# A two-block transformer kernel: engine queues ordered by a timeline simulation

## The chip, the cores and the metric

The kernel runs on one core of a Trainium2 chip. The metric is the device time of one execution in microseconds (us); the profile comes from one further execution on the same kind of chip. The core's engines are named as in the profile: PE (matrix multiply, with PEld for its weight loads), DVE (vector), ACT (scalar and activation), POOL (GpSimd), and SP, which only issues DMAs. Each engine works through its own queue in a fixed order.

## What is computed

Two blocks follow one another on 512 tokens of width 1024, in float32. Cut to what matters:

```python
# first block
h = modulate(rms_norm(x, norm1_g), shift1, scale1)
q, k, v, g_ret, u, sv, gate_a, gate_b = split(h @ w_in)
branch_a = (silu(g_ret) * head_norm(retention(rotary(q), rotary(k), v))) @ w_ret_out
branch_b = spatial_gating(gelu(u), gelu(sv)) @ w_sgu_out
x = x + gate1 * ((sigmoid(gate_a) * branch_a + sigmoid(gate_b) * branch_b) @ w_out)
h2 = modulate(rms_norm(x, norm2_g), shift2, scale2)
x = rms_norm(x + gate2 * peer(h2), final_g)
# peer, per token: top 16 of 128 x 128 experts in each of 8 heads
act = gelu(h2 . expert_u[expert]) * softmax(top_s)
out = sum(act * expert_v[expert])
# second block, two layers: window attention, latent attention and a gated
# convolution, merged; a context of 256 tokens goes through the first layer
```

## The kernel before

Every float32 product is made of three fp32r products: an operand is split into a high part (ACT, line 105) and a low part (POOL or DVE, line 107), and PE adds high x high, low x high and high x low (lines 80 to 82). Weights stream in over SP's queue (`load`, line 72) into small rings of buffers, are split, and are used once.

The work has these stages. The profile's times for them are rounded to 100 us.

- `first_mixer` (to about 550 us) and then `experts`. In `experts` three streams of work are written into one another. `route` finds the 16 experts of each head. `up_products` multiplies the first 384 tokens by all 16,384 rows of `expert_u` (tile `u`, weights `wr`, `wh`, `wl`, result `hb`). `context` runs the 256 context tokens through the first layer of the second block (tile `cm`, weights `wrc`, `whc`, `wlc`).
- The last 128 tokens are handled differently (`gathered`, line 663 on). For each of 128 (head, rank) pairs POOL issues a gather of one row per token from `expert_u` and one from `expert_v` (line 684, 256 gathers, 128 x 1024 each) into `sg`, a ring of `SG = 4` buffers. A DVE operation reads each: a dot product (line 197) for an `expert_u` row, and an addition into `sacc` (line 699) for an `expert_v` row. A buffer is free for the next gather when its DVE operation is done.
- From about 1900 us the loop over `expert_v` runs: 32 rounds of four weight tiles `vr`, split on ACT and DVE, eight accumulators `acc` on PE (lines 594 to 625), until about 2500 us.
- `second` runs the two layers of the second block (2500 us to the end): per layer, window attention with the convolution's and the gates' products written into it, latent attention, gates, merge.

What sets the order of the queues: the kernel is written with the Tile framework. The source emits instructions in one program order. The author interleaves streams in it by hand with counters: `tick(R1)` to `tick(R6)` emit a part of a filler stream for each step of a main stream, and `sparse(S2)`, `sparse(S3)`, `sparse(S4)`, `sparse(SU)`, `sparse(S5)` (lines 656 to 661) emit one gather step for each unit of due count. `S5 = 0.85` per weight tile of the `expert_v` loop asks for 0.85 x 128 = 109 of the 256 steps inside that loop, if that many are left. When the context closes, Tile plays the whole program through a simulator with a clock: each time an engine is free in that simulation, it is given, of its instructions whose inputs are ready and whose buffers are free, the one that comes first in the source. The order in which each engine received its instructions becomes its queue. So the simulator's clock decides where the queues leave the source's order. On the chip the queue is fixed: an instruction that is not ready holds up all that stands behind it on its engine.

The context is opened in `kernel`, line 1819; `body` calls `Kern(...).build()`.

## Time and profile before

| what | us |
|---|---|
| median of 3 runs | 3908.92 (3907.82 to 3917.36) |
| the profiled execution's own time | 3920.43 |
| its span, first to last instruction | 3918.7 |
| PE busy in the span | 3484.4 (89%) |
| DVE busy | 2363.8 (60%) |
| POOL busy | 1622.9 (41%) |
| ACT busy | 1590.1 (41%) |

The profiled execution is 11.5 us longer than the median of the runs, and 1.7 us longer than its span. Durations below come from that execution. A wait in the profile is the idle time of an engine ahead of an instruction, put down to what ended it. `x` counts instructions. The granted clock of PE is given as a share of its full rate.

### The profile page before, as it was taken

The page shows a single profiled execution, that of the slowest core. Times are in us where ns is not written, and L with a number is a line of the kernel's source. Part 1 is how long each engine was busy: PE and PEld are TensorE (multiplying, and loading weights), DVE is VectorE, ACT ScalarE, POOL GpSimd, SP SyncE. Part 2 cuts the span into 40 slices and gives each one's busy share as a digit, 9 for nine tenths or more (in the row PEclk, how much of TensorE's full clock was granted, in tenths as well). Part 3 has the DMA queues.
Part 4 walks back from the last instruction along what each step waited for, and adds up shares of the span by engine and source line. Part 5 has one row for each costly group of instructions (what it writes and reads, how often), then busy time and mean ns, then how long its engine had stood idle before and what let it go on. Part 6 is the DMA issues. An engine that isn't in the chain of part 4 may idle for free.

```text
span 3918.7 us, 54792 instructions
## 1 busy us (share of the span) xinstructions
PE 3484.4 (89%) x20243; PEld 3124.0 (80%) x20243; DVE 2363.8 (60%) x4567; ACT 1590.1 (41%) x2976; POOL 1622.9 (41%) x1248
## 2 busy tenths in 40 slices
PE   5999999979878777768999999699999998999998
PEld 4888787878768776767899999687877787777787
DVE  7556545799878786876377555544425554442554
ACT  3322233336633354443433333344426643452563
POOL 4454544451256777675300000155424435543342
PEclk9999999989989887888999999699999998999999
DMA  6346324347888886776789766222221232212113
GB/s 240 132 176 249 124 92 146 107 148 278 295 292 283 315 267 234 274 243 229 257 310 324 244 222 215 77 82 70 66 74 51 89 110 72 71 65 77 50 61 107
DMA packets 271947, 667.91 MB, mean 170 GB/s; under 512 B 25280, under 2 KB 87104, under 8 KB 268736
## 3 DMA queue, kind: packets, MB, share of 16 engines
q1 hardware_dynamic: 219248, 469.30, 35.0%
q0 software_dynamic: 36864, 134.23, 10.1%
q10 hardware_dynamic: 15568, 60.89, 4.1%
q8 instruction: 159, 2.61, 0.3%
q14 instruction: 108, 0.88, 0.1%
HBM read 601.34 MB, written 62.98 MB: 170 GB/s over the span
## 4 chain that ended last, share of the span: by engine, by line
PE 56%; DVE 14%; DMA 10%; issue 9%; POOL 5%; ACT 4%; SPq 0%; POOLq 0%; DVEq 0%; ACTq 0%
PE mm L80 5%; PE mm L81 5%; PE mm L82 5%; PE acc L82 4%; PE acc L81 4%; PE acc L80 4%; PE gm L80 3%; PE gm L81 3%; PE gm L82 3%; DMA sg<-ev,xid 3%; POOL sg L684 2%; PE pv L1083 2%; DMA sg<-ur,xid 2%; POOL wl L107 2%; PE tp L1053 2%
## 5 line engine op out<-in xcount | busy, mean ns | idle before, releaser
L107 POOL TENSOR_TENSOR wl<-wr,wh 128x512 fp32r<-128x512 f32 (+3 forms) x418 | 687.0, 1660 | 472.8 <-ACT wh L105 459.9
L105 ACT CAST wh<-wr 128x512 fp32r<-128x512 f32 (+4 forms) x536 | 348.0, 666 | 512.6 <-PE mm L81 169.7
L80 PE MATMUL u<-hh,wh 128*128 128x384 f32 (+1 forms) x1032 | 369.8, 358 | 34.3 <-ACT hb L711 32.2
L82 PE MATMUL u<-hh,wl 128*128 128x384 f32 (+1 forms) x1032 | 366.2, 355 | 28.6 <-POOL wl L107 16.8
L81 PE MATMUL u<-hl,wh 128*128 128x384 f32 (+1 forms) x1032 | 363.0, 352 | 0.0
L81 PE MATMUL acc<-al,vh 128*128 128x384 f32 (+2 forms) x1056 | 353.1, 335 | 0.1
L82 PE MATMUL acc<-ah,vl 128*128 128x384 f32 (+2 forms) x1056 | 353.0, 335 | 0.0
L80 PE MATMUL acc<-ah,vh 128*128 128x384 f32 (+2 forms) x1056 | 352.8, 335 | 0.0
L105 ACT CAST vh<-vr 128x1024 fp32r<-128x1024 f32 x128 | 134.7, 1052 | 344.3 <-DMA vr<-ev 227.8
L80 PE MATMUL mm<-hh,wh 128*128 128x512 f32 (+2 forms) x608 | 242.0, 401 | 33.1 <-ACT wh L105 23.6
L107 DVE TENSOR_TENSOR vl<-vr,vh 128x1024 fp32r<-128x1024 f32 x128 | 158.5, 1239 | 168.5 <-ACT vh L105 158.8
L684 POOL DMA_INDIRECT sg<-ur,xid x128 | 169.6, 1325 | 213.7 <-DVE sg L197 155.2
L81 PE MATMUL mm<-hl,wh 128*128 128x512 f32 (+2 forms) x608 | 243.2, 400 | 3.3 <-POOL hl L107 3.1
L82 PE MATMUL mm<-hh,wl 128*128 128x512 f32 (+2 forms) x608 | 242.4, 399 | 1.4 <-POOL wl L107 1.4
L80 PEld LDWEIGHTS u<-hh,wh 128*128 128x128 f32 x1032 | 206.9, 201 | 39.0 <-ACT hb L711 34.5
L898 POOL TENSOR_TENSOR acc<-acc,sf 128x256 f32<-128x256 f32 x8 | 6.0, 754 | 558.5 <-ACT sf L895 550.3
L82 PEld LDWEIGHTS u<-hh,wl 128*128 128x128 f32 x1032 | 205.3, 199 | 35.2 <-POOL wl L107 20.2
L197 DVE SCALAR_TENSOR_TENSOR wm<-wm,row 128x1024 f32<-128x1024 f32 x120 | 183.0, 1538 | 72.1 <-DMA wm<-wmod 57.4
L699 DVE SCALAR_TENSOR_TENSOR sacc<-sg,wts,sacc 128x1024 f32<-128x1024 f32 x128 | 189.0, 1476 | 50.4 <-DMA sg<-ev,xid 49.6
L80 PE MATMUL cm<-ch,whc 128*128 128x256 f32 (+1 forms) x584 | 178.0, 306 | 46.0 <-DVE cmt L970 17.5
L684 POOL DMA_INDIRECT sg<-ev,xid x128 | 166.5, 1301 | 125.8 <-DVE sacc L699 84.0
L197 DVE SCALAR_TENSOR_TENSOR sg<-sg,htok 128x1024 f32<-128x1024 f32 x128 | 178.7, 1397 | 59.4 <-DMA sg<-ur,xid 59.3
(726 smaller groups left out, 10256.1 us busy)
## 6 DMA issues: line engine op xcount, KB each, us to landing
wr<-eu SPq DMA_DIRECT2D x256, 256.0 KB, 3.4
vr<-ev SPq DMA_DIRECT2D x128, 512.0 KB, 4.5
wm<-wmod SPq DMA_DIRECT2D x88, 512.0 KB, 5.7
wrc<-w SPq DMA_DIRECT2D x83, 512.0 KB, 5.3
wr<-wA SPq DMA_DIRECT2D x80, 512.0 KB, 4.0
wr<-w SPq DMA_DIRECT2D x156, 256.0 KB, 2.6
wrg<-w SPq DMA_DIRECT2D x104, 256.0 KB, 2.6
hd<-hb ACTq DMA_DIRECT2D x64, 384.0 KB, 4.1
```

What stands on the lines that cost most here:

```text
L80: mm(ps, lh, rh, start=first, stop=False)
L81: mm(ps, lh, rl, start=False, stop=False)
L82: mm(ps, ll, rh, start=False, stop=last)
L105: nc.scalar.copy(hi, x)
L107: eng.tensor_tensor(lo, x, hi.bitcast(F32), op=OP.subtract)
L197: self.nc.vector.scalar_tensor_tensor(chunk, chunk, 1.0, row, op0=OP.mult, op1=OP.mult, accum_out=dst)
L684: nc.gpsimd.indirect_dma_start(t, None, tabs[i], bass.IndirectOffsetOnAxis(idx[:, j:j + 1], 0))
L699: nc.vector.scalar_tensor_tensor(acc, t, wts[:, j:j + 1], acc, op0=OP.mult, op1=OP.add)
L898: eng.tensor_tensor(acc[1], acc[1], sf, op=OP.add)
L1053: nc.tensor.transpose(t[:, (b - i) * 128:(b - i + 1) * 128], p[:, b * 128:(b + 1) * 128], self.ident)
L1083: nc.tensor.matmul(o[:, lo:hi], v(b), pt[k][:, b, lo:hi], start=i == 0 and k == 0, stop=i == len(parts) - 1 and k == 1)
```

## The change

```diff
@@ -1816,7 +1816,7 @@
     nc = bacc.Bacc("TRN2", target_bir_lowering=False, num_devices=1)
     a = {n: nc.dram_tensor(n, v.shape, mybir.dt.from_np(v.dtype), kind="ExternalInput").ap() for n, v in arrays.items()}
     out = nc.dram_tensor("out", (128, 8, T), F32, kind="ExternalOutput").ap()
-    with tile.TileContext(nc) as tc:
+    with tile.TileContext(nc, schedule_with_timeline_sim=True) as tc:
         body(tc, a, out, {})
     r = run_bass_kernel_spmd(nc, [arrays], core_ids=[0])
     y = r.results[0]["out"]
```

One argument is added. The source of the program, its tiles, rings and instructions stay as they are. The simulation that gives each engine its order is played on Tile's timeline simulator in place of its plain one. The library calls the timeline simulator the more detailed of the two: it keeps occupancy for engines, sequencers and DMA engines, and it counts a fixed cost of POOL's elementwise instructions that the plain one leaves out. Each queue's order, the buffer that each tile gets, and the semaphore waits that follow from both are worked out anew.

## Rows read from the trace of the kernel before

**Rows 1.** The page: busy time, share of the span and instructions, by engine.

```profile
PE 3484.4 (89%) x20243; PEld 3124.0 (80%) x20243; DVE 2363.8 (60%) x4567; ACT 1590.1 (41%) x2976; POOL 1622.9 (41%) x1248
```

**Rows 2.** Busy time by stage: window, length, engines, granted PE clock, DMA share, GB/s.

```profile
0.00:100.00 100.00, 60.30 (x266) 47.36 (x267) 75.31 (x123) 35.17 (x51) 48.06 (x27) 0.95 0.65 242
100.00:900.00 800.00, 736.74 (x4050) 653.98 (x4049) 503.15 (x1366) 242.93 (x388) 381.47 (x193) 0.95 0.42 147
900.00:1900.00 1000.00, 785.03 (x5192) 738.11 (x5191) 756.70 (x1117) 455.04 (x806) 568.98 (x444) 0.89 0.78 270
1900.00:2500.00 600.00, 590.67 (x3401) 589.07 (x3402) 367.97 (x546) 217.07 (x319) 32.54 (x26) 0.98 0.72 247
2500.00:2600.00 100.00, 64.87 (x444) 60.24 (x444) 40.34 (x99) 35.31 (x72) 45.32 (x39) 0.77 0.30 100
2600.00:3918.00 1318.00, 1246.77 (x6895) 1035.25 (x6895) 620.30 (x1318) 604.60 (x1343) 546.56 (x521) 0.98 0.23 74
```

**Rows 3.** The same table for 1100 to 1900 us alone.

```profile
1100.00:1900.00 800.00, 610.40 (x3855) 577.02 (x3853) 580.09 (x835) 331.82 (x637) 528.49 (x411) 0.88 0.76 264
```

**Rows 4.** The same table for instructions on `sg` alone: DVE, then POOL.

```profile
900.00:1900.00 1000.00, 359.96 (x374) 324.31 (x247) 0.89 0.78 270
1900.00:2500.00 600.00, 0.00 (x0) 0.00 (x0) 0.98 0.72 247
```

**Rows 5.** Longest waits of 900 to 1900 us: total us, times, longest.

```profile
POOL sg L684 <- DVE sg L197: 154.8, 39, 22.9
POOL sg L684 <- DVE sacc L699: 99.0, 35, 14.3
...
DVE sg L197 <- DMA sg<-ur,xid: 59.3, 31, 7.3
...
DVE sacc L699 <- DMA sg<-ev,xid: 49.6, 26, 5.0
```

**Rows 6.** Tile `sg`, 900 to 1900 us: ns min/median/max, first and last start; landing.

```profile
L684 POOL DMA_INDIRECT sg<-ev,xid x128: 933/1119/2278, 951.2 to 1803.5; - x128
L699 DVE SCALAR_TENSOR_TENSOR sacc<-sg,wts,sacc x128: 1264/1283/6228, 1001.2 to 1812.6; 128x1024 f32<-128x1024 f32 x128
L197 DVE SCALAR_TENSOR_TENSOR sg<-sg,htok x123: 1203/1221/5260, 912.8 to 1759.6; 128x1024 f32<-128x1024 f32 x123
...
DMA to landing us min/median/max: 4.1/6.3/12.8
```

**Rows 7.** Instructions in order of time, 1560 to 1570 us: start, us, what, wait.

```profile
1563.32 0.94 POOL L684 DMA_INDIRECT sg<-ev,xid  x1 [0.30 <-issue]
...
1567.09 1.28 DVE L699 SCALAR_TENSOR_TENSOR sacc<-sg,wts,sacc 128x1024 f32<-128x1024 f32 x1 [5.00 <-DMA sg<-ev,xid]
...
1568.29 0.41 DVE L972 SCALAR_TENSOR_TENSOR u<-u,cm 128x256 f32<-128x256 f32 x1
...
1568.65 0.94 POOL L684 DMA_INDIRECT sg<-ev,xid  x1 [3.14 <-DVE sacc L699]
...
1568.76 0.39 PE L80 MATMUL cm<-ch,whc 128*128 128x256 f32 x1 [0.64 <-DVE u L972]
```

**Rows 8.** The chain that ended last, 900 to 1900 us, shares by line.

```profile
by line: issue 27.1%; DMA sg<-ev,xid 12.4%; POOL sg L684 7.3%; DMA sg<-ur,xid 6.8%; DMA wrc<-w 5.6%; DVE sacc L699 3.8%; POOL wl L107 3.7%; DVE wlc L107 3.5%; DVE sg L197 3.1%; PE u L81 2.2%; PE u L82 2.2%; PE u L80 2.1%; DMA wr<-eu 1.7%; P
```

**Rows 9.** Waits of PE, 900 to 1900 us.

```profile
PE cm L82 <- DVE wlc L107: 30.1, 22, 7.2
...
PE cm L80 <- DVE u L972: 14.9, 6, 4.2
```

**Rows 10.** Low-part splits of `wr` on POOL and DVE, 900 to 1900 us: ns min/median/max.

```profile
L107 POOL TENSOR_TENSOR wl<-wr,wh x106: 1252/1302/2335, 1117.4 to 1899.1; 128x512 fp32r<-128x512 f32 x106
L107 DVE TENSOR_TENSOR wl<-wr,wh x62: 675/684/1755, 902.2 to 1119.3; 128x512 fp32r<-128x512 f32 x62
```

**Rows 11.** Busy time of the 100 us that moved the most bytes.

```profile
2000.00:2100.00 100.00, 100.00 (x579) 100.00 (x578) 75.68 (x114) 33.64 (x46) 0.00 (x0) 1.00 0.92 321
```

**Rows 12.** The longest wait of PE, 2600 to 3918 us.

```profile
PE tp L1053 <- DVE pt L107: 7.3, 15, 1.4
```

## The prediction

> **What bounds the kernel now.** I began with the page: PE is busy for 3484 of 3919 us [rows 1], so no order of the queues can return more than about 434 us, the time that PE stands still, plus what it loses at a lower clock. The table by stage says where that time lies [rows 2]. From 900 to 1900 us PE is busy for 785 of 1000 us at a mean granted clock of 0.89; this stage holds 215 us of the 434. The loop over `expert_v` (1900 to 2500 us) keeps PE busy for 591 of 600, and the second block from 2600 us for 1247 of 1318. The first 900 us leave 103 us, 40 of them in the first 100, where the first loads and the norm must come before any product. So a new order has one large place to win, 900 to 1900 us, and it can lose anywhere.
>
> What holds that stage? No engine is full by its busy time: from 1100 to 1900 us DVE has 580 of 800 us, POOL 528, PE 610, and the DMA engines 0.76 [rows 3]. The list of waits explains the rest [rows 5]. POOL stands for 154.8 + 99.0 = 254 us in front of a gather, because the DVE operation that frees the buffer in the ring of four hasn't run. With its 528 busy us, POOL's queue is taken for some 780 of those 800 us (a few of the 254 lie before 1100). DVE in turn stands for 59.3 + 49.6 = 109 us in front of an operation on `sg` whose gather hasn't landed. The tile view gives the loop its numbers: POOL 1.1 us for a gather, a landing of 6.3 us in the median and up to 12.8, DVE 1.2 to 1.3 us [rows 6]. The chain agrees: 12.4 + 6.8 = 19.2% of the stage's chain, 192 us, is spent in gathers on their way [rows 8].
>
> One stretch shows how this reaches PE [rows 7]. A gather is issued at 1563.32. DVE's next instruction is the addition that needs it, and DVE stands for 5.00 us until 1567.09. Behind it in DVE's queue is `u` (L972), a product of the context's gate, 0.41 us long; PE's next context product waits for that `u`. POOL's next gather waits 3.14 us for the buffer, and the sum of the context's result stands behind that gather. The order was drawn with a clock on which the gather had landed by then.
>
> A second view shows the same. The source asks for 109 of the 256 gather steps inside the loop over `expert_v` (0.85 for each of 128 weight tiles). In the trace that loop has none: all of `sg`'s 360 us on DVE and 324 us on POOL in this table lie before 1900 us [rows 4], the last addition at 1812.6 [rows 6]. The plain clock showed DVE and POOL free and the gathers landed, and the planner pulled the steps forward.
>
> **The change, part by part.** No instruction, tile or DMA is added or removed; only orders, buffers and waits are redrawn. The sum is therefore made of waits.
>
> (1) *Gathers against the rest, 900 to 1900 us.* A clock that keeps the DMA engines occupied, beside 270 GB/s of other and own traffic in this stage [rows 2], lands a gather later than one that gives each transfer the engines to itself. Then at 1562 us the planner sees the addition not ready, and gives DVE the `u` of the context instead. It also issues fewer gathers early, so fewer stand in POOL's queue in front of splits. POOL's splits have a price of their own: 1.30 us for a `wl` piece that takes DVE 0.68 [rows 10]; a clock that counts POOL's fixed cost also sees POOL fuller than before. The most that this returns is what DVE lost, 109 us; POOL's 254 us are the same stalls seen further down the ring, and aren't added. The least is nothing, or a loss (the rivals). I take half, 54 us: PE's own waits on the two DVE results that stand in this jam, `wlc` and `u`, are 30.1 + 14.9 = 45 us [rows 9], and the chain's 192 us in landings says that the stalls are mostly on the path. The next thing late would be DMA: the stage moves 270 MB, and at the 321 GB/s of the busiest slice [rows 11] that takes 841 us, so there is room for 54.
>
> (2) *Steps that move into the loop over `expert_v`.* Each brings 1.25 us of DVE, 1.1 of POOL and 0.52 MB. POOL has 567 us free there and DVE 232 [rows 2]. Up to some 60 steps (75 us of DVE, 31 MB) the DMA rate would rise from 247 to (148 + 31) MB / 600 us = 298 GB/s, under the busiest slice. I count nothing; the cover is PE's own work, and if it is gone the price is the second rival's.
>
> (3) *The other stages.* PE idles 71 us in the second block, its longest single wait there being 7.3 us in 15 pieces [rows 12], 9 us in the `expert_v` loop, 35 us around 2550, 63 us from 100 to 900. A better clock could return part; a different one can lose. I take 0, with plus 71 and minus 35 (half of the 71) as ends.
>
> Sum: 3920.4 - 54 = 3866 us against the profiled execution's own time. That execution is 11.5 us above the median of the runs, so I forecast 3855 us.
>
> A rule of the Trainium skill speaks against part (1). The page "DMA: Bandwidth & Descriptors", section "Anatomy of one DMA — SWDGE (gpsimd) path", puts one such transfer at 2.0 us plus its bytes over 436 GB/s, which is 3.2 us by estimate for a gather of 524 kB; the trace has 6.3 us [rows 6], so in this stage the measurement is twice the rule. A clock built on that rule alone would keep most of the stalls, and the sum would stay near 3909.
>
> **The rivals.**
>
> *The stalls stay.* If the new clock too lands gathers before the chip does, the same coupling of ring, POOL and DVE comes out in another order. For it: 6.3 us is the median, and the longest landing is twice that, which no planned time meets. Against it: DVE's 57 waits are of 1.9 us on average, so a shift of two us in the planned landing removes half of them. Time: 3909, within 12.
>
> *Filler spent early.* This is the one on the other side. In the second block PE is 95% busy because products of gates and of the convolution are ready whenever the attention chain (scores, maximum, exponential, transposes, values) is not. The planner takes whatever is ready. If its clock makes the chain's steps ready later, or commits filler sooner, the filler is gone before the chain ends and PE then waits at each step. The price: with little filler, from 1100 to 1900 us, PE is 76% busy [rows 3]; in the second block a fall from 95% to 90% already doubles the 71 us of idle time. Time: 3909 + 71 = 3980. For it: the exposed stretch at 2500 to 2600 has PE at 65% and clock 0.77 [rows 2]. Against it: the longest wait there totals only 7.3 us [rows 12], and rings of two weight buffers keep filler from running far ahead. It decides once PE falls below about 94% from 2600 us on.
>
> *Gathers crowd the loop over `expert_v`.* With all 109 steps there, (148 + 57) MB at 321 GB/s take 639 us instead of 600, and PE, now full, would wait for `vr`. Plus 39 us, less anything won before: 3948 if nothing is. For it: the source asks for exactly that. Against it: DVE and POOL are idle enough before 1900 us for any work-conserving planner to pull steps forward.
>
> *The change doesn't do what it says.* The two clocks could agree on every choice that matters. Against it: the present order already leaves the source's by 109 steps on the clock's word alone, so another clock will choose otherwise somewhere. Time: 3909.
>
> **How the numbers follow.** A measurement of this kernel can tell about 0.3%, 12 us, from no change. The forecast (stalls partly gone, 3855) gets 0.50: the waits are there, named, and of the kind that a clock with busy DMA engines would see. The stalls staying gets 0.12 and the change doing nothing 0.02: together 0.14 for the same time. Filler spent early gets 0.25, the crowded loop 0.11: together 0.36 for slower. The forecast's own range runs from 3909 - 109 - 35 = 3765 to 3897. The whole range has that low end, with some 7% below it, and reaches up to the filler rival's 3980, with about 12% above it.
>
> **What would show it.** Right: between 900 and 1900 us DVE's waits for gathers (109 us) and POOL's for the ring (254 us) at half or less; operations on `sg` after 1900 us; PE above 80% in that stage, and the `expert_v` loop starting some 50 us sooner. Wrong: those two waits as long as before; PE below 94% in the second block; or PE waiting for `vr` in the loop.

## The result, and the profile after

**4037.5 us against 3910.7: slower, ratio 1.0327, 95% interval 1.0295 to 1.0359.** The forecast was 3855, the range ended at 3980. The profiled execution took 4040.19 us, its span 4038.2.

The page of the kernel after, busy time by engine [rows 1]:

```profile
PE 3521.8 (87%) x20243; PEld 3168.4 (78%) x20243; DVE 2401.0 (59%) x4567; ACT 1558.8 (39%) x2948; POOL 1612.3 (40%) x1248
```

Span less busy time is what PE stood still: 516 us after, 434 before. So 82 of the 119.5 us of span are new idle time, and in 37 PE is busy longer with the same 20243 matmuls. By stage, in the windows of [rows 2]:

```profile
900.00:1900.00 1000.00, 794.57 (x5168) 743.99 (x5166) 803.05 (x1096) 423.86 (x770) 583.81 (x443) 0.88 0.75 259
1900.00:2500.00 600.00, 546.76 (x3132) 542.21 (x3133) 366.26 (x558) 204.75 (x287) 4.42 (x6) 0.95 0.72 248
...
2600.00:4038.00 1438.00, 1309.09 (x7038) 1098.48 (x7037) 645.32 (x1341) 613.91 (x1364) 552.83 (x531) 0.94 0.21 69
```

From 2600 us on PE is 91.0% busy instead of 94.6%, and the clock fell from 0.98 to 0.94. Counted by landmarks: the loop over `expert_v` has its first product 14 us later (1964.4 instead of 1950.2), ends another 17 later, and the second block takes 88 us longer. The second block alone, before and then after:

```profile
2502.00:3919.00 1417.00, 1309.64 (x7330) 1093.49 (x7329) 659.69 (x1414) 639.10 (x1413) 591.88 (x559) 0.97 0.23 76
2533.00:4038.00 1505.00, 1346.60 (x7323) 1134.73 (x7322) 671.91 (x1408) 639.55 (x1417) 587.67 (x560) 0.93 0.22 72
```

PE stands still there for 158 us instead of 107, and the 37 us of longer matmuls are all here, at a mean clock of 0.93 instead of 0.97.

Yet the waits that the prediction wanted shorter are shorter. Waits of 900 to 1900 us [rows 5]:

```profile
POOL sg L684 <- DVE sacc L699: 67.2, 37, 4.6
...
POOL sg L684 <- DVE sg L197: 60.3, 32, 5.8
...
DVE sacc L699 <- DMA sg<-ev,xid: 27.1, 20, 3.7
...
DVE sg L197 <- DMA sg<-ur,xid: 20.4, 21, 2.4
```

DVE's 109 us in front of gathers became 47.5, POOL's 254 us for the ring 127.5. A landing takes 6.6 us in the median, so the chip didn't get faster; the order is better spaced. (The Trainium skill, "DMA: Bandwidth & Descriptors", "Anatomy of one DMA — SWDGE (gpsimd) path", would put such a transfer at 3.2 us by estimate; this trace, like the one before, has about twice that.) It gave nothing: from the first router product (`uq`, at 589 us before and 596 after) to the loop over `expert_v` the kernel takes 1368 us instead of 1361. PE's waits for `wlc` and `u` did fall, from 30.1 and 14.9 us [rows 9], but others grew. From 596 to 1964 us after:

```profile
PE u L82 <- POOL wl L107: 29.8, 19, 4.6
...
PE ct L147 <- DVE sqa L174: 21.7, 2, 18.7
...
PE cm L82 <- DVE wlc L107: 7.8, 10, 2.1
...
PE cm L80 <- DVE u L972: 0.3, 1, 0.3
```

In all, PE waits 246 us there for other engines, and 249 before. Other work was put in the place of the stalls. What the up-products `u` and the one-hot products `gps` do on PE shows it; here the kernel after, by tile (ns min/median/max, first and last start in us):

```profile
L82 PE MATMUL u<-hh,wl x1032: 272/337/691, 618.2 to 1538.1; 128*128 128x384 f32 x169, 128*128 128x256 f32 x2, 128*128 128x128 f32 x1
```

```profile
L865 PE MATMUL gps<-ow,oh x768: 215/219/331, 1037.5 to 1264.1; 128*128 128x128 f16 x192
```

and the same two in the kernel before:

```profile
L82 PE MATMUL u<-hh,wl x1032: 273/337/689, 610.1 to 1950.1; 128*128 128x384 f32 x169, 128*128 128x256 f32 x2, 128*128 128x128 f32 x1
```

```profile
L865 PE MATMUL gps<-ow,oh x768: 216/219/330, 893.4 to 1125.6; 128*128 128x128 f16 x192
```

The up-products, which lie beside the context's chain until 1950 us before, are used up at 1538 us, and the chain (its last product starts at 1943 us) runs on without them. Busy time after, while there are up-products and when there are none:

```profile
1100.00:1540.00 440.00, 379.29 (x2644) 358.84 (x2644) 382.31 (x428) 200.40 (x315) 318.16 (x228) 0.93 0.84 296
1540.00:1940.00 400.00, 255.39 (x1596) 231.79 (x1596) 250.01 (x459) 148.01 (x337) 144.16 (x139) 0.75 0.53 176
```

PE falls from 86% to 64%, and the granted clock from 0.93 to 0.75 of full speed. And the one-hot products start 144 us later. Of these, 42 lie ahead of the last router value; in the others DVE did other things first. DVE's costliest groups between the last router value and the first one-hot product (794 to 1038 us) after the change:

```profile
L197 DVE SCALAR_TENSOR_TENSOR sg<-sg,htok 128x1024 f32<-128x1024 f32 x40 | 51.6, 1291 | 5.7 <-DMA sg<-ur,xid 5.6
L107 DVE TENSOR_TENSOR wl<-wr,wh 128x512 fp32r<-128x512 f32 x70 | 46.6, 680 | 4.0 <-ACT wh L105 3.9
L699 DVE SCALAR_TENSOR_TENSOR sacc<-sg,wts,sacc 128x1024 f32<-128x1024 f32 x23 | 30.4, 1320 | 0.2 <-DMA sg<-ev,xid 0.2
```

In the same stretch before (752 to 893 us) the like groups are:

```profile
L197 DVE SCALAR_TENSOR_TENSOR sg<-sg,htok 128x1024 f32<-128x1024 f32 x5 | 6.0, 1215 | 0.0
...
L107 DVE TENSOR_TENSOR wl<-wr,wh 128x512 fp32r<-128x512 f32 x5 | 3.2, 679 | 0.8 <-ACT wh L105 0.8
```

So the gather steps didn't move later, as the prediction had it; they moved in between the router and the one-hot products.

### The profile page after: what moved, and what is told of

Read it like the earlier page. It is cut to its first block, busy times and chain, and to the rows that moved or that the text cites. A ratio compares the mean times of both kernels' runs of the same rounds, so it can differ in the third digit from the quotient of the medians.

```text
span 4038.2 us, 54766 instructions
## 1 busy us (share of the span) xinstructions
PE 3521.8 (87%) x20243; PEld 3168.4 (78%) x20243; DVE 2401.0 (59%) x4567; ACT 1558.8 (39%) x2948; POOL 1612.3 (40%) x1248
## 5 line engine op out<-in xcount | busy, mean ns | idle before, releaser
L107 POOL TENSOR_TENSOR wl<-wr,wh 128x512 fp32r<-128x512 f32 (+3 forms) x418 | 677.3, 1639 | 419.9 <-ACT wh L105 372.9
L105 ACT CAST wh<-wr 128x512 fp32r<-128x512 f32 (+4 forms) x536 | 339.7, 667 | 535.5 <-PE mm L81 130.2
L80 PE MATMUL u<-hh,wh 128*128 128x384 f32 (+1 forms) x1032 | 361.1, 350 | 18.0 <-ACT hb L711 13.6
L82 PE MATMUL acc<-ah,vl 128*128 128x384 f32 (+2 forms) x1056 | 312.3, 332 | 0.0
L107 DVE TENSOR_TENSOR pt<-tp,pt 128x384 fp32r<-128x384 f32 (+2 forms) x256 | 127.9, 503 | 223.6 <-ACT pt L105 220.3
L684 POOL DMA_INDIRECT sg<-ev,xid x128 | 190.5, 1488 | 126.3 <-DVE sacc L699 61.8
L80 PEld LDWEIGHTS acc<-ah,vh 128*128 128x128 f32 x1056 | 201.2, 191 | 39.4 <-issue 18.8
L81 PEld LDWEIGHTS u<-hl,wh 128*128 128x128 f32 x1032 | 202.4, 196 | 0.4
L81 PEld LDWEIGHTS acc<-al,vh 128*128 128x128 f32 x1056 | 201.7, 191 | 0.0
```

Of the source, the lines that this page charges most:

```text
L80: mm(ps, lh, rh, start=first, stop=False)
L81: mm(ps, lh, rl, start=False, stop=False)
L82: mm(ps, ll, rh, start=False, stop=last)
L105: nc.scalar.copy(hi, x)
L107: eng.tensor_tensor(lo, x, hi.bitcast(F32), op=OP.subtract)
L684: nc.gpsimd.indirect_dma_start(t, None, tabs[i], bass.IndirectOffsetOnAxis(idx[:, j:j + 1], 0))
```

## The experiments

All kernels but the first four and p_rates_up use one method. The program is drawn once with the clock whose order is wanted (the plain one; for g_p_pe_time the timeline one) and thrown away; the second drawing, with the clock named, has the queue of an engine tied to the recorded order, by edges that set an order and no wait:

```
+    def pin(self, engine, order, lo, hi):
...
+        own = {i.name: i for i in self.nc.cur_bb.bb.instructions[lo:hi] if i.engine == engine}
+        names = [n for n in order if n in own]
+        for a, b in zip(names, names[1:]):
+            self.tc.add_manual_dep(own[b], a, dep, reason="order")
...
+        self.pin(mybir.EngineType.PE, ORDER.get('PE'), m[0], m[4])
```

The marks m[0] to m[4] are the start, the start of the experts' stage, the loop over `expert_v`, the second block and the end. Line numbers of these kernels are up to 30 higher than above. Ratios are to the kernel before, which was run beside each (medians of 3917 to 3920 us); one hundredth is 39 us.

**1. TensorE in the source's order.** The first theory (A) was the prediction's own rival: PE takes filler early, and the source's order would hold it back. Each TensorE instruction is tied behind the TensorE instruction that the source issued before it, in the second block, in the experts' stage, or both; the last kernel does it with the plain clock.

```
+        n = self.here()
         self.second()
+        self.pin(mybir.EngineType.PE, n)
...
+            self.pin(mybir.EngineType.PE, n0)    # n0: where the router starts
```

> Timeline clock as in the changed kernel, but in the second block every TensorE instruction is tied behind the one the source issued before it; all other engines are ordered freely. Theory A (the clock lets PE take the products of gates and convolution early, and they are missing later): the 89 us that the second block lost (46 in window attention of layer 0, 7 in its latent part and merge, 36 in window attention of layer 1) come back, 4037 - 89 = 3950, within 15; PE's waits for pt in front of a transpose fall from 35 us to about 7. Theory B (the order of DVE, ACT or POOL in the block makes pt late, whatever PE does): within 15 of 4037, and PE's waits for pt stay above 25 us.

Measured: 4287.7 us, ratio 1.0944 (1.0919 to 1.0969).

> Timeline clock, but from the first router product to the last up-product every TensorE instruction is tied behind the one the source issued before it; the second block stays as the changed kernel has it. Theory A (up-products spent early, the context chain left bare): u runs again until about 1900 us, and the 14 us by which the loop over expert_v starts later come back, so 4023; if the halved stalls at the gathers are worth what the prediction took for them, another 54 come off, 3969. Theory B (PE's order is not what binds there, the gathers and DVE are): within 15 of 4037.

Measured: 4188.4 us, 1.0689 (1.0660 to 1.0718).

> Both ties together, timeline clock. Theory A: 4037 - 89 - 14 = 3934 if the gather stalls are worth nothing, down to 3880 if they are worth the 54 us of the prediction. Theory B: within 20 of 4037.

Measured: 4430.7 us, 1.1312 (1.1287 to 1.1336).

> Both ties, but with the plain clock (the kernel before with TensorE tied to the source's order in the same two stretches). Control: theory A says that the plain clock keeps PE near the source's order in the second block, so little changes there; in the experts' stage it moved some products by hundreds of places. 3911, within 25. If it is well below that, the source's order of PE is better than either clock's, and what t_pe_both gains is not the timeline clock's.

Measured: 4415.8 us, 1.1278 (1.1253 to 1.1304).

No expectation was met in any of the four. The source's order is no reference: on either clock it ends some 500 us above the kernel before. One thing is worth keeping: with PE in the same fixed order in both stretches, the two clocks are 15 us apart.

**2. TensorE in the plain clock's order.** The reference has to be the order that the plain clock draws. Theory A2: the loss lies in PE's order as the timeline clock draws it, against the plain clock's.

```
+        self.pin(mybir.EngineType.PE, ORDER.get('PE'), m[0], m[4])    # g_t_pe_plain; clock: timeline
+        self.pin(mybir.EngineType.PE, ORDER.get('PE'), m[0], m[4])    # g_p_pe_time; clock: plain, ORDER: timeline
+        self.pin(mybir.EngineType.PE, ORDER.get('PE'), m[1], m[2])    # g_t_pe2_plain; clock: timeline
+        self.pin(mybir.EngineType.PE, ORDER.get('PE'), m[3], m[4])    # g_t_pe3_plain; clock: timeline
```

> Timeline clock, but TensorE's whole queue is tied to the order that the plain clock draws for it (all of its instructions stand as in the kernel before); DVE, ACT, POOL and SP are ordered by the timeline clock round it. Theory A2 (the 3.3% lie in TensorE's order alone): 3911, within 12; with the shorter gather stalls worth something besides, down to 3857. Theory B (the order of the other engines carries the loss): above 3990.

Measured: 3998.6 us, 1.0210 (1.0189 to 1.0230).

> The mirror: plain clock, but TensorE's whole queue tied to the order that the timeline clock draws for it. Theory A2: 4037, within 15. Theory B: within 30 of 3911. If both this kernel and its mirror lie in the middle, near 3975, the loss is in how the engines' orders fit each other and belongs to no one queue.

Measured: 4130.2 us, 1.0552 (1.0526 to 1.0579).

> Timeline clock, TensorE tied to the plain clock's order only from the first router product to the last up-product; the second block as in the changed kernel. Theory A2: the 14 us that the stages before the loop over expert_v lost come back, 4023; if the halved gather stalls (109 to 48 us on DVE) are worth what the prediction took, 54 more, 3969. Theory B: 4037, within 12.

Measured: 4032.7 us, 1.0293 (1.0271 to 1.0316).

> Timeline clock, TensorE tied to the plain clock's order only in the second block; the stages before as in the changed kernel. Theory A2 (products of gates and convolution taken early): the 89 us of the second block come back, 3948, within 12, and TensorE's waits for pt before a transpose fall from 35 us to about 7. Theory B: 4037, within 12.

Measured: 4005.6 us, 1.0217 (1.0196 to 1.0238).

Theory A falls in its strict form: putting PE's order back takes off 1.2 of the 3.3 hundredths, nearly all of it in the second block. In the experts' stage, where the filler was visibly spent, it takes off 0.3, and the two intervals overlap. This is also the test of the prediction's 54 us. With PE's queue as before, the up-products last until 1980 us again, and DVE's waits for gathers stay short; 900 to 1980 us of g_t_pe_plain:

```profile
DVE sacc L720 <- DMA sg<-ev,xid: 33.1, 22, 6.9
...
DVE sg L200 <- DMA sg<-ur,xid: 23.7, 20, 3.5
```

57 us instead of 109, and the loop over `expert_v` starts at 1980, 30 us later than before (12 of the 30 are there at the first router product already). So halved stalls didn't make this stage shorter. What they are worth alone isn't shown, because DVE still has 50 gather steps between the last router value and the first one-hot product (754 to 961 us), and PE, in its old order, now waits for the router's results. Among its longest waits of 601 to 1980 us:

```profile
PE tps L849 <- DVE kt L835: 43.0, 2, 23.6
PE gps L886 <- DVE ow L877: 34.3, 26, 4.4
...
PE tps L849 <- DVE tv L674: 20.8, 1, 20.8
```

These are 98 us, where the kernel before has 9.

In the second block the wait that theory A named did go, and others came in its place. PE's longest waits from 2600 us on, after:

```profile
PE tp L1053 <- DVE pt L107: 35.5, 42, 1.9
PE tp L1053 <- DVE sz L1076: 10.1, 6, 3.1
```

and in the same way from 2600 us on with PE's order put back in that block (g_t_pe3_plain):

```profile
PE tp L1074 <- DVE nb L1058: 14.5, 14, 1.6
PE sc L159 <- DVE rs2y L145: 12.5, 6, 6.2
PE pv L1104 <- ACT pt L108: 8.5, 23, 0.6
PE tp L1074 <- DVE pt L110: 7.9, 8, 1.4
```

`pt` in front of a transpose falls from 35.5 to 7.9 us, as expected; `nb`, `rs2y` and ACT's `pt` now come late. PE stands in the plain clock's order and waits for engines that don't; its clock is back at 0.98 from 2600 us on.

The mirror (g_p_pe_time) speaks against a loss that belongs to any one queue: PE in the new order and the rest drawn round it by the plain clock is worse than both whole kernels.

**3. The other queues.** Theory C: every queue takes filler early. Theory D: only a misfit between queues.

```
+        self.pin(mybir.EngineType.DVE, ORDER.get('DVE'), m[0], m[4])    # g_t_dve_plain, g_t_pe_dve_plain, g_t_other_plain
+        self.pin(mybir.EngineType.PE, ORDER.get('PE'), m[0], m[4])    # g_t_pe_dve_plain
+        self.pin(mybir.EngineType.Activation, ORDER.get('Activation'), m[0], m[4])    # g_t_act_plain, g_t_other_plain
+        self.pin(mybir.EngineType.Pool, ORDER.get('Pool'), m[0], m[4])    # g_t_other_plain
```

> Timeline clock, DVE's whole queue tied to the plain clock's order, all other engines free. Theory C (each queue takes filler early, not PE's alone: on DVE 63 gather steps, 82 us, and 70 splits of up-product weights, 47 us, stand between the last router value and the first one-hot product, where the kernel before has 5 and 5): the first one-hot product comes back from 1038 to about 900 us, the loop over expert_v ends at 2502 instead of 2533, and the second block keeps at least what PE's order costs there (39 us); between 3956 and 4006. Theory D (no queue's order is at fault alone, only the misfit of a tied queue and free ones): 4037 or above.

Measured: 4221.2 us, 1.0778 (1.0758 to 1.0797).

> Timeline clock, TensorE's and DVE's whole queues tied to the plain clock's orders, ACT, POOL and SP free. Theory C: the two queues carry the whole loss, 3918, within 15. If ACT's or POOL's order holds the 81 us that remained with TensorE tied alone: above 3970.

Measured: 3983.7 us, 1.0163 (1.0143 to 1.0183).

> Timeline clock, ACT's whole queue tied to the plain clock's order, all others free. ACT rounds every weight tile and reads out most products, so filler can't run further ahead on PE or DVE than ACT lets it; PE then stands a mean of 17 places from the plain clock's order instead of 324, DVE 7 instead of 29. Theory C (the loss is filler taken hundreds of places early): most of the 119 us come back, 3918 to 3960. If small swaps of neighbouring steps cost as much as the long moves: 3980 or above.

Measured: 4238.5 us, 1.0819 (1.0797 to 1.0842).

> Timeline clock, DVE, ACT and POOL tied to the plain clock's orders, only TensorE and SP free. Theory C: TensorE has no room left to take filler early, so 3918 to 3950. Theory D or the first theory A2 in its strict form (TensorE's own choices cost whatever the others do): 3980 or above.

Measured: 4200.3 us, 1.0722 (1.0703 to 1.0741).

Theory C's numbers fail everywhere, and the bounds set for theory D are met, though D names no mechanism. Three kernels in which PE was free and some other queue tied are worse than the change itself, though in the last two PE stands a mean of only about 16 places from the good order (at most some 500), against hundreds in the change: the mean distance doesn't tell the cost. With DVE tied the one-hot products did come back (from 1038 to 921 us) and it didn't help. And with PE and DVE as before, 1.6 hundredths remain, though ACT stands a mean of 1.2 places, POOL 0.7 and SP 1.0 from the plain clock's order.

**4. What is left, by queue, and a control.**

```
+        self.pin(mybir.EngineType.PE, ORDER.get('PE'), m[0], m[4])    # all three
+        self.pin(mybir.EngineType.DVE, ORDER.get('DVE'), m[0], m[4])    # all three
+        self.pin(mybir.EngineType.Activation, ORDER.get('Activation'), m[0], m[4])    # g_t_all_plain, g_t_pda_plain
+        self.pin(mybir.EngineType.Pool, ORDER.get('Pool'), m[0], m[4])    # g_t_all_plain, g_t_pdps_plain
+        self.pin(mybir.EngineType.SP, ORDER.get('SP'), m[0], m[4])    # g_t_all_plain, g_t_pdps_plain
```

> Timeline clock, all five queues tied to the plain clock's orders. Control: the buffers and orders are those of the kernel before, and only which of the DMA semaphores some 60 transfers signal on is drawn anew. If the change acts through the orders alone: 3918, within 12. If something else that the timeline clock writes into the program costs time: well above, near the 3984 of the kernel with TensorE and DVE tied.

Measured: 3918.6 us, 1.0001 (0.9988 to 1.0015). The change acts through the orders, and what follows from them, and through nothing else that the runs can tell.

> TensorE, DVE and ACT tied to the plain clock's orders, POOL and SP free (they stand a mean of 0.2 and 0.7 places from it). With TensorE and DVE tied alone 65 us remained. If these lie in ACT's order: 3918, within 15. If in SP's and POOL's: 3970 or above.

Measured: 3934.4 us, 1.0043 (1.0031 to 1.0055), just above the 3933 expected if ACT's order holds the rest.

> The complement: TensorE, DVE, POOL and SP tied, only ACT free (a mean of 1.0 place from the plain clock's order, at most 54). If the 65 us lie in ACT's order: 3970 or above. If in SP's and POOL's: 3918, within 15. If both kernels lie between, the two share it.

Measured: 3974.4 us, 1.0150 (1.0133 to 1.0168).

ACT's order alone costs 1.5 hundredths, with every other queue exactly as before. POOL and SP together cost 0.4; the two weren't told apart. The profiled executions differ by 24.7 us: the loop over `expert_v` takes 17 longer and the second block 15, and 8 are gained ahead of the loop. The trace shows one place: in the first 200 us of the loop over `expert_v`, PE's busy time with all tied,

```profile
1944.00:2144.00 200.00, 199.72 (x1151) 199.04 (x1149) 147.67 (x221) 67.37 (x92) 0.00 (x0) 1.00 0.92 319
```

and with SP and POOL free (g_t_pda_plain),

```profile
1936.00:2136.00 200.00, 189.45 (x1064) 185.27 (x1063) 132.48 (x200) 61.11 (x84) 0.00 (x0) 0.99 0.81 285
```

PE stands still for 10 us there. A likely cause, not tested by itself, is SP's order: its list has the loop's first two `vr` loads 7 places earlier than before and its first `gt` and `ht` 17 to 21, among the last up-product weights; the DMA engines then move 285 GB/s instead of 319 in the stretch in which the loop asks most of them.

**5. Is the kernel before just a narrow optimum?** Theory E: its rates were chosen under the plain clock, and any redrawn order costs per cents.

```
-R1, R2, R3, R4, R5, R6 = 0.6, 0.7, 0.7, 0.38, 0.9, 0.12
+R1, R2, R3, R4, R5, R6 = 0.63, 0.735, 0.735, 0.399, 0.945, 0.126
-S2, S3, S4, SU, S5 = 0.0, 0.6, 0.9, 1.2, 0.85
+S2, S3, S4, SU, S5 = 0, 0.63, 0.945, 1.26, 0.8925
```

> Plain clock; all the filler rates of the source (R1 to R6 and S3 to S5, SU) multiplied by 1.05, nothing else. It tells whether the kernel before sits in a narrow optimum, so that any redrawn order costs per cents (theory E): then 3945 or above. If the loss is the timeline clock's own (theories C and D): within 15 of 3918.

Measured: 3911.5 us, 0.9989 (0.9979 to 1.0000). Theory E falls for these rates, moved up by 5%: the plain clock redraws the order and loses nothing.

**6. Which of ACT's moves?** Comparing the ACT lists of g_t_pdps_plain and of the kernel before, 291 weight roundings (`wh`, `whg`, `whc`) stand earlier, and what stands later is mostly read-outs of PSUM (`pt` 104, `hb` 87, `stg` 68, `u` 59). Theory F: a rounding in front of a read-out delays PE. Both kernels tie PE, DVE, POOL and SP; for ACT:

```
+            if engine == mybir.EngineType.Activation and b not in self.rounds:    # a_rounds_tied
+                continue
...
+        if engine == mybir.EngineType.Activation:    # a_rounds_free
+            names = [n for n in names if n not in self.rounds]
```

> As the kernel in which only ACT is free (58 us slower than before), but a weight rounding on ACT (wh, whc, whg, who) may not overtake the instruction that the plain clock puts before it; all other ACT work is free. Theory F (the timeline clock puts roundings of the next weights ahead of read-outs of PSUM that PE waits for: 291 roundings stand earlier there, and pt, hb, stg and u later): most of the 58 us come back, 3918 to 3935. If the order of the attention's own ACT steps (exponential, p, pt) holds them: 3955 or above.

Measured: 3917.9 us, 0.9992 (0.9980 to 1.0005).

> The complement: all of ACT's work but the weight roundings keeps the plain clock's order among itself, the roundings go where the timeline clock puts them; TensorE, DVE, POOL and SP tied. Theory F: 3974, within 15, with ACT standing some 98 us in front of roundings whose up-product weights haven't landed, as with all of ACT free. Otherwise: 3935 or below.

Measured: 3974.0 us, 1.0136 (1.0115 to 1.0158).

Theory F holds from both sides: with the four other queues tied, the place of the roundings carries ACT's loss. With the roundings held back, the other moves of ACT that remain (among them 57 `pt`) cost nothing; with only the roundings free, nearly the whole loss is there. One number of the expectation missed: ACT stands 79 us in front of up-product weights that haven't landed, not 98, and 70 with the roundings tied. Waiting for weights is therefore not the main mechanism; that a rounding runs first is. The instructions in order of time in a_rounds_free, 2638 to 2641 us:

```profile
2638.26 1.14 ACT L109 CAST whg<-wrg 128x512 fp32r<-128x512 f32 x2 [2.96 <-PE gm L85]
2638.29 0.49 PE L1083 MATMUL tp<-c_ident,p 128*128 128x128 f32 x3
...
2639.30 0.59 ACT L966 ACTIVATE sz<-gm 128x512 f32<-128x512 f32 x1
...
2639.79 0.47 ACT L109 CAST pt<-tp 128x384 fp32r<-128x384 f32 x1
...
2640.31 0.39 PE L1113 MATMUL pv<-pt,va 128*128 128x256 f32 x1 [0.48 <-ACT pt L109]
```

and the same work in a_rounds_tied, 2628 to 2631 us:

```profile
2628.54 0.62 ACT L109 CAST whg<-wrg 128x512 fp32r<-128x512 f32 x1 [2.98 <-PE gm L85]
2628.57 0.49 PE L1083 MATMUL tp<-c_ident,p 128*128 128x128 f32 x3
...
2629.07 0.59 ACT L966 ACTIVATE sz<-gm 128x512 f32<-128x512 f32 x1
...
2629.56 0.47 ACT L109 CAST pt<-tp 128x384 fp32r<-128x384 f32 x1
2629.92 0.63 ACT L109 CAST whg<-wrg 128x512 fp32r<-128x512 f32 x1
2630.08 0.39 PE L1113 MATMUL pv<-pt,va 128*128 128x256 f32 x1
```

With the roundings free, ACT takes two pieces of the next weight, 1.14 us, before it reads out a gate (`sz`) and the transposes (`pt`). PE runs out of other products and stands for 0.48 us until `pt` is there. With the roundings tied, the second piece stands behind `pt`, and PE doesn't wait. PE waits for `pt` in front of `pv` 28 times with the roundings free, and 4 times with them tied (3 of the 28 are there in both). In 24 of the 28 a rounding is among the three instructions of ACT ahead of `pt`. PE's wait from 2514 us on in a_rounds_free,

```profile
PE pv L1113 <- ACT pt L109: 13.0, 28, 1.6
```

and from 2508 us on in a_rounds_tied:

```profile
PE pv L1113 <- ACT pt L109: 2.4, 4, 0.9
```

Summed over the lists of PE's waits of the whole span, PE waits for ACT 152.8 us in the one and 110.0 in the other: 43 us, beside 38 us between the two spans (3965.8 and 3927.4). Of these 43, `pv` for `pt` is 11, the up-products for `hb` 10 and the one-hot products for `stg` 6. The sum goes with the time only roughly: the kernel before, as fast as a_rounds_tied, has 134.6, with less waiting for POOL in its place. By span less busy time, PE stands still 31 us longer with the roundings free.

## Why the prediction was wrong

**Part (1), gathers against the rest: mechanism found, worth nothing.** The waits fell to half, as the forecast said, and PE's waits for `wlc` and `u`, by which the 54 us were priced, fell from 45 to 8. The step from waits to time failed: "I take half, 54 us". It took PE's other waits as fixed. They grew by as much, so that PE waited 246 us for other engines instead of 249, and the stage took 7 us longer. With DVE's stalls at 57 us and PE's queue as before, the loop began 30 us later, not 54 sooner, with PE waiting for the router instead (experiment 2). The direction was wrong too. The prediction had fewer steps ready early and some moved into the loop over `expert_v`. They moved forward instead: 63 steps and 70 splits, 129 us of DVE, in front of the work that the one-hot products wait for.

**Part (2), steps that move into the loop: nothing, as forecast, for another reason.** None moved there. Still, the loop takes 17 us longer, 569 instead of 552, and nearly as much, 570, with only POOL and SP free (553 with all tied). Those two queues cost 0.4 hundredths, which no part counted.

**Part (3), the other stages: this is the term that failed most.** It was taken as 0, with a loss of 35 us as its end, because the second block shows PE 95% busy and no wait over 7.3 us [rows 12]. Those rows say that there is little to gain; I read them as little to lose. It cost 88 us, 51 of standing still and 37 of matmuls at a lower clock; the clock was in no term. The chain there hands a step between PE, ACT and DVE every microsecond or so, and in the traces above one rounding of half a microsecond ahead of a read-out was enough to make PE wait.

**The rivals.** *Filler spent early* had the right sign and place in the second block, and its own criterion was met (PE at 91.0%, below 94%). Its price, 71 us of idle time, was above the 51 measured and left out the 37 of the clock, and PE's queue was only part of it. Taking the queues back in turn gives the account of the 3.3 hundredths: PE's order 1.2, DVE's 0.5, ACT's 1.2, POOL's and SP's 0.4. It holds for this succession only; the mirror and the kernels of experiment 3 show that the terms don't add in another. The prediction thought of filler as products on PE. On ACT the filler is weight roundings, and it never priced that queue. The rival's argument against itself, that rings of two weight buffers keep filler close, fails for the same reason: one buffer ahead is enough to put a rounding in front of a read-out.

*The stalls stay* is refuted by the waits, the crowded loop by the place of the gathers, and *the change doesn't do what it says* by the orders. At what time the new clock takes a gather for landed isn't shown by any run; only that the stalls halved.

**What stays open.** Why the timeline clock puts roundings, gather steps and up-products earlier isn't shown; only that it does, and what it costs. How the orders of PE and DVE cost their 1.2 and 0.5 is shown at most by the waits above, not by a test of single steps as for ACT. Why four kernels with some queues tied and the rest redrawn are worse than either clock (1.055 to 1.082) isn't shown either. Holding only ACT's roundings back in the changed kernel, with all else free, wasn't tried. No kernel here beats the one before.

## What to carry to other kernels

A halved wait is not yet time: ask what the freed engine takes up next, and whether that stands in front of something. When a planner draws the queues, look for its filler on every engine, not on TensorE alone. On ScalarE, holding weight roundings behind the read-outs of PSUM that the matmuls wait for was worth 1.4 hundredths here, with the other queues tied. To find which queue carries a loss, tie queues to the other plan's order cumulatively, and end with all of them tied as a control; a single tied queue can mislead.

## What was not expected

ACT got lighter and the kernel slower. The new clock groups functions better: 43 loads of activation tables became 15. Two of the groups before,

```profile
L711 ACT ACT_TABLE_LOAD x18 | 23.1, 1283 | 0.4
L1039 ACT ACT_TABLE_LOAD x15 | 19.2, 1283 | 0.8 <-DVE nb L1037 0.6
```

and after:

```profile
L711 ACT ACT_TABLE_LOAD x4 | 5.1, 1283 | 0.1
L1039 ACT ACT_TABLE_LOAD x3 | 3.8, 1283 | 0.9 <-DVE nb L1037 0.8
```

28 loads of 1283 ns are 36 us of ACT, and its busy time fell by 31. (The Trainium skill, "ScalarE: Activation LUTs", section "What ACT_TABLE_LOAD costs", counts a drain besides and gives about 2.66 us for a switch, 74 us for 28 by estimate. The 1283 ns agree with the rows; no row here shows the drain as idle time.) ACT is 39% busy: how much it does matters less than what it does first.

TensorE's clock took its share as well: its mean over the span fell from 0.946 to 0.926. The 37 us that this cost lie in the second block, as shown above. The clock is lower still from 1540 to 1940 us, but little was lost there as a whole: from the first router product to the loop PE is busy 1103 us after and 1099 before. The mean of 0.75 in that stretch lies halfway between the two levels (1.2 and 2.4 GHz), and it fell to that when PE, 86% busy until then, became 64% busy.
